# Loading the first tile of an interleave kernel by eight 16-row DMAs

## The chip, the cores and the metric

The kernel runs on one core of a Trainium2 chip. Times are device microseconds. A time quoted for a kernel is the median of its unprofiled runs; a "span" is that of one profiled run and is some 2 us shorter. A "row" below is one packet of 32 KiB: one partition of a tile, moved by one of the core's 16 DMA engines. SBUF is the on-chip memory that holds the tiles, HBM the memory off the core that holds x, y and the result.

## The reference

```python
batch, seq, dim = 32, 256, 1024          # x and y: float32, 32 MiB each
result = np.zeros((batch, seq, dim * 2), dtype=np.float32)
result[..., 0::2] = x
result[..., 1::2] = y
```

There is no arithmetic: 64 MiB are read and 64 MiB written.

## The kernel before

```python
P, WL, WS = 128, 8192, 4096
xpool, ypool, opool = ...                # two buffers each          [cut]
nc.vector.memset(zero, 0.0)              # 16x128
nc.scalar.dma_start(out=first, in_=zero) # 8 KB into out; overwritten later
for lw in lwidths:                       # eight tiles of 128 x 8192
    xs = dataclasses.replace(xf, offset=start, ap=[[lw, P], [1, lw]])
    ys = ...                                                        # [cut]
    nc.sync.dma_start(out=xtile, in_=xs) # 4 MiB, 128 rows of 32 KiB
    nc.sync.dma_start(out=ytile, in_=ys)
    while soff < lw:                     # two halves of 4096 columns
        nc.vector.tensor_copy(out=otile[:, 0::2], in_=xsub)
        nc.vector.tensor_copy(out=otile[:, 1::2], in_=ysub)
        nc.scalar.dma_start(out=os_, in_=otile)   # 4 MiB
```

After compiling, the very first load is moved ahead of the barrier at the program's start. Loads go through SyncE's queue (q1), stores through ScalarE's (q10); both use the same 16 DMA engines (2304 and 2336 packets, 49.9% and 49.5% of the engines' time in the span).

## Time and profile before

| | before |
|---|---|
| median of the first five runs | 315.93 us (315.54 to 316.48) |
| span of the profiled run | 313.8 us |
| DMA engines busy | 99.4% of the span |
| rows for each DMA engine | 256, of 1.213 us each: 310.5 us |
| first x tile landed, first y tile landed | 12.27 us, 21.97 us |

### The profile page before, as it was taken

How to read it: one execution, taken by the hardware profiler on the slowest of the kernel's cores; microseconds unless marked ns; L12 is line 12 of the kernel's file. 1: busy time of each engine (PE TensorE's matmuls, PEld its weight loads, DVE VectorE, ACT ScalarE, POOL GpSimd, SP SyncE). 2: the span in 40 equal slices, each digit the busy share in tenths (PEclk: the TensorE clock that was granted, in tenths of full speed). 3: DMA queues.
4: the chain of work that ended last, by engine and by line, in shares of the span. 5: the costliest groups of instructions: out<-in, count | busy, mean ns of one | idle time of the engine just before them, and what ended most of it. 6: DMA issues, size and time to landing. Idle time of an engine off the chain costs nothing.

```text
span 313.8 us, 152 instructions
## 1 busy us (share of the span) xinstructions
DVE 72.8 (23%) x33; POOL 0.2 (0%) x4
## 2 busy tenths in 40 slices
DVE  0433002231032410325003150130501305023500
POOL 0000000000000000000000000000000000000000
DMA  8999999999999999999999999999999999999997
GB/s 339 464 405 397 468 401 464 405 464 405 464 405 464 405 459 409 451 418 451 418 434 434 430 439 426 443 413 455 401 468 401 468 401 468 401 468 401 464 405 334
DMA packets 4640, 134.23 MB, mean 428 GB/s; under 512 B 528, under 2 KB 544, under 8 KB 544
## 3 DMA queue, kind: packets, MB, share of 16 engines
q1 hardware_dynamic: 2304, 67.11, 49.9%
q10 hardware_dynamic: 2336, 67.12, 49.5%
HBM read 67.11 MB, written 67.12 MB: 428 GB/s over the span
## 4 chain that ended last, share of the span: by engine, by line
DMA 83%; DVE 11%; DVEq 1%; issue 0%
DMA out_dram<-otile 76%; DMA ytile<-in_y_dram 7%; DVE otile L71 6%; DVE otile L70 5%; DVEq L83 1%; DVEq L70 0%
## 5 line engine op out<-in xcount | busy, mean ns | idle before, releaser
L70 DVE COPY otile<-xtile 128x4096 f32<-128x4096 f32 x16 | 36.6, 2295 | 184.9 <-DMA out_dram<-otile 173.7
L71 DVE COPY otile<-ytile 128x4096 f32<-128x4096 f32 x16 | 36.6, 2292 | 39.8 <-DMA ytile<-in_y_dram 39.8
L45 DVE MEMSET zero<- 16x128 f32 x1 | 0.2, 165 | 0.9 <-PEq L119 0.9
L119 POOL MEMSET const-bfloat16-1.0<- 128x1 bf16 x1 | 0.1, 102 | 0.0
L119 POOL MEMSET const-uint8-127<- 128x1 uint8 x1 | 0.1, 102 | 0.0
L119 POOL MEMSET const-float32-0.0<- 128x1 f32 x1 | 0.1, 99 | 0.2 <-issue 0.2
L119 POOL MEMSET const-float32-1.0<- 128x1 f32 x1 | 0.1, 99 | 0.0
## 6 DMA issues: line engine op xcount, KB each, us to landing
out_dram<-otile ACTq DMA_DIRECT2D x16, 4096.0 KB, 29.1
xtile<-in_x_dram SPq DMA_DIRECT2D x8, 4096.0 KB, 43.6
ytile<-in_y_dram SPq DMA_DIRECT2D x8, 4096.0 KB, 60.7
out_dram<-zero ACTq DMA_DIRECT2D x1, 8.0 KB, 6.3
```

The source lines that it names most:

```text
L45: nc.vector.memset(zero, 0.0)
L70: nc.vector.tensor_copy(out=otile[:, 0::2], in_=xsub)
L71: nc.vector.tensor_copy(out=otile[:, 1::2], in_=ysub)
L83: tc.compile()
L119: nc = _bacc.Bacc("TRN2", target_bir_lowering=False, num_devices=1)
```

## The change

The first x tile is loaded by eight DMAs. Each has one row for each DMA engine: 16 rows run at a time while x is loaded, and each group of 16 is followed by 16 completion writes. The intent, as the form of the pieces suggests, is that all 16 engines have work after one short DMA and start together. The r-th DMA takes partitions r, 8+r, ... 120+r. Only the first of the eight is moved ahead of the barrier; in the changed kernel's trace SyncE issues the second at 1.21 us.

```diff
-        nc.sync.dma_start(out=xtile, in_=xs)
+        if start == 0:
+            for r in range(P // 16):
+                nc.sync.dma_start(
+                    out=xtile.rearrange("(e r) w -> e r w", r=P // 16)[:, r],
+                    in_=xs.rearrange("(e r) w -> e r w", r=P // 16)[:, r],
+                )
+        else:
+            nc.sync.dma_start(out=xtile, in_=xs)
```

## The prediction

> **What bounds the kernel now.** The kernel moves 64 MiB in and 64 MiB out and has VectorE interleave each pair of tiles in between. I read the page first: the busy shares, the slices, the queues. Then the chain of waits in order of time, then the waits of VectorE, then the issues of SyncE, then windows of the start, and last the records of single DMA packets in the trace, which the page only sums.
>
> The page, its parts 1 to 3:
>
> ```profile
> span 313.8 us, 152 instructions
> ...
> DVE 72.8 (23%) x33; POOL 0.2 (0%) x4
> ...
> DMA  8999999999999999999999999999999999999997
> GB/s 339 464 405 397 468 401 464 405 464 405 464 405 464 405 459 409 451 418 451 418 434 434 430 439 426 443 413 455 401 468 401 468 401 468 401 468 401 464 405 334
> DMA packets 4640, 134.23 MB, mean 428 GB/s; under 512 B 528, under 2 KB 544, under 8 KB 544
> ...
> q1 hardware_dynamic: 2304, 67.11, 49.9%
> q10 hardware_dynamic: 2336, 67.12, 49.5%
> ```
>
> VectorE is busy 23% of the span, the 16 DMA engines 99.4% (the shares of the two queues added), from the first slice to the last. 4640 packets less the 544 small ones are 4096, one for each row of 32 KiB of a tile, so 4096 / 16 = 256 rows for each DMA engine. In the records of single packets, all but a few dozen of these rows take 1.213 us, loads and stores alike: 32768 B / 1.213 us = 27.0 GB/s an engine, 432 GB/s for 16. And 256 x 1.213 = 310.5 us of the span of 313.8. The other 3.3 us are the start (first row at 0.99 us), the longer first row and the completion after the last row (it ends at 312.7). So what binds is the rows that each DMA engine has to work off one after another, and nothing later can make up for time that an engine loses.
>
> The chain in order of time, its first pieces:
>
> ```profile
> by line: DMA out_dram<-otile 76.3%; DMA ytile<-in_y_dram 6.8%; DVE otile L71 5.7%; DVE otile L70 5.1%; DVEq L83 0.7%; issue 0.2%; DVEq L70 0.0%
> ...
> 0.78 21.19 DMA ytile<-in_y_dram
> 21.97 0.02 issue
> 22.00 4.51 DVE otile L71 x2
> 26.50 0.02 issue
> 26.53 40.87 DMA out_dram<-otile
> ```
>
> The chain runs through the first y tile, which queues behind the first x tile on the same 16 engines: x's semaphore is complete at 12.27 us, y's at 21.97, 9.7 us = 8 rows x 1.213 apart. The reader is to see that the chain names y though half of its 21 us is x's transfer. VectorE's waits:
>
> ```profile
> DVE otile L70 <- DMA out_dram<-otile: 173.7, 14, 21.6
> DVE otile L71 <- DMA ytile<-in_y_dram: 39.8, 8, 5.2
> DVE otile L70 <- DMA xtile<-in_x_dram: 11.3, 1, 11.3
> ```
>
> VectorE waits for x only once, 11.3 us at the start: that is the transfer which is changed. SyncE's issues:
>
> ```profile
> 0.00 0.37 SPq L56 DMA_DIRECT2D xtile<-in_x_dram  x1
> 0.78 0.33 SPq L57 DMA_DIRECT2D ytile<-in_y_dram  x1
> 1.16 0.42 SPq L56 DMA_DIRECT2D xtile<-in_x_dram  x1
> 1.63 0.51 SPq L57 DMA_DIRECT2D ytile<-in_y_dram  x1
> 16.80 0.33 SPq L56 DMA_DIRECT2D xtile<-in_x_dram  x1
> ```
>
> An issue costs 0.33 to 0.51 us of SyncE; four tiles are queued by 2.1 us, so the engines are fed for 39 us. And the windows of x's transfer and of y's:
>
> ```profile
> 1.40:11.10 9.70, 0.00 (x0) 0.00 (x0) 1.00 0.91 389
> 11.10:20.80 9.70, 4.50 (x2) 0.00 (x0) 1.00 1.00 432
> ```
>
> (The last two columns are DMA share and GB/s.) y moves at 432 GB/s, x at nearly that from its second row on. Only x's first row is odd: the 16 engines start it between 0.99 and 1.93 us and end it between 2.86 and 3.43, so a row takes 1.5 to 2.3 us here, and the stagger of 0.6 us stays in the later rows.
>
> [...] the small store of 16 rows of zeros has 16 packets of 512 B, and they stand at the row boundaries of 16 different engines (5.27, 5.45, 5.46 us and on). So eight DMAs of 16 rows give each engine eight rows again. [...]
>
> **The change part by part.** Removed: one load of 128 rows. Added: eight of 16 rows, the r-th taking partitions r, 8+r, 16+r, ... 120+r.
>
> - Ports. [...] a row takes 2 x 1.213 = 2.43 us, the eight rows 19.4 in place of 9.7: +9.7 us.
> - [...] with leads of up to 0.6 us I allow -0.2.
> - The first row. [...] If the stagger of 0.6 us halves, the slowest engine gains 0.3: -0.3.
> - Seven more semaphore writes for each engine, some 6 ns each between rows in the records: +0.04.
> - Issues: seven more, 7 x 0.33 to 0.5 = 2.3 to 3.5 us of SyncE, which starts them at 0.78. An engine's first row ends at 2.9 at the earliest and the second DMA is issued at 0.8 to 1.2: fed in time, 0.
> - Waits: the built program has eight completion semaphores in rotation, so the eighth x piece now waits for the first to land, and the first y load waits for the store of zeros (landed 6.3 us after its issue, at 7.4). Six or seven rows per engine are queued meanwhile: 0.
>
> Sum: +9.7 - 0.2 - 0.3 + 0.04 = +9.2 us. All of it lies on the path: DVE's first copy waits for x, y is behind x in the same rings, and the engines are full to the end. So 316.2 + 9.2 = 325.4 us.
>
> **The rivals.**
>
> - Ports don't bind, or buffering hides them: a row stays at 1.21 us. For it: the intent of the change, and that this trace shows no conflict. [...] Time: 316.2 - 0.3 = 315.7 to 316.3.
> - [...]
> - The new waits take over: y's load isn't issued until zeros have landed. If the zeros have their turn after five slow rows, 5 x 2.43 + 1 = 13 us, it is still ahead of x's end at 21. Only if they landed after x's last row would the engines go dry, for 1 to 2 us: 317 to 318 without the port effect.
> - Reads at a pitch of 256 KiB in HBM collide. [...] not expected; it would look like the port effect, but for partition order alone wouldn't matter.
>
> **Range and chances.** The port effect, shared evenly, has some 70%: 324 to 326.5. Partial or unfair sharing some 8%: 319 to 323. No effect, or only starvation at the start, some 22%: 315.5 to 318. Over 2% slower means above 322.5, so slower 0.73, same 0.25, faster 0.02. A range that holds eight in ten has to reach from inside the unlikely low group: 317 to 327.
>
> **What would show it.** Right: x rows of about 2.4 us in the packet records until 21 us; around 216 GB/s at an undiminished DMA share in a window from 3 to 20 us; VectorE's first copy at 21.5 to 22 us and not 12.3, its first copy of y 9.7 us later, near 31.5; the first big store 9 us late; the same shift in each later piece of the chain, and y rows and all later rows at 1.213 again. Wrong: x rows of 1.21 us with the first copy near 12 us (no port limit); half of the engines with fast rows [...]; a gap in the packets between x and y (the semaphore wait); or a shift at the start that shrinks towards the end, which would mean that the engines had slack after all.

The sum came to +9.7 - 0.2 - 0.3 + 0.04 = +9.2 us, on 316.2 us for the kernel before. The factor of 2 on the measured row of 1.213 us and the 0.2 us given back for leads were assumptions, as the halving of the stagger in the third term was. The other two terms leave -0.3 us, or 315.9 us in all. "Port", here and in the expectations below, is only a name for the supposition that the rows of a 16-row piece slow each other where they are written; what would do that, no trace shows. A rival at about 321 us, to which the range of 319 to 323 us belongs, is cut as a whole.

## The result

The changed kernel takes 325.83 us (325.71 to 326.10, five runs) against 315.93 us; the ratio is 1.0315, with a 95% interval from 1.0301 to 1.0329. Ratios here are the mean time of one kernel's fast runs over that of the other's fast runs of the same rounds, so not quite the ratio of the medians quoted. It is slower by 9.9 us; the spans of the two profiled runs (323.65 and 313.85 us) differ by 9.8.

The page of the changed kernel, parts 2 and 3:

```profile
DMA  9999999999999999999999999999999999999997
GB/s 195 211 259 437 450 409 437 454 413 429 454 437 405 454 441 401 454 445 405 445 450 409 437 450 409 437 454 429 413 454 441 401 454 445 405 445 445 405 445 324
DMA packets 4752, 134.23 MB, mean 415 GB/s; under 512 B 640, under 2 KB 656, under 8 KB 656
...
q1 hardware_dynamic: 2416, 67.11, 51.3%
q10 hardware_dynamic: 2336, 67.12, 48.0%
```

The DMA engines look as busy as before, yet the first two slices of the GB/s line show half the rate: a busy engine is not a fast one. The bytes are the same; 112 more small packets are the completion writes of seven more DMAs on 16 engines. Windows of the start:

```profile
1.40:11.10 9.70, 0.06 (x1) 0.00 (x0) 1.00 0.98 207
11.10:20.80 9.70, 0.00 (x0) 0.00 (x0) 1.00 1.00 206
20.80:30.50 9.70, 4.50 (x2) 0.00 (x0) 1.00 1.01 416
```

Before, the first two windows moved 389 and 432 GB/s. Half the rate ends with x's rows, which on the 16 engines end between 20.95 and 22.03 us. VectorE's waits:

```profile
DVE otile L79 <- DMA out_dram<-otile: 172.9, 14, 20.9
DVE otile L80 <- DMA ytile<-in_y_dram: 39.6, 8, 5.2
DVE otile L79 <- DMA xtile<-in_x_dram: 21.5, 1, 21.5
```

Only the single wait for x has grown, from 11.3 to 21.5 us; the others stand within 0.8 us. The start of the chain, asked for the first 40 us:

```profile
1.21 0.09 issue
1.29 0.18 DVE zero L45
1.47 0.02 issue
1.49 8.64 DMA out_dram<-zero
10.13 0.02 issue
10.15 22.44 DMA ytile<-in_y_dram
32.59 0.02 issue
32.61 4.51 DVE otile L80 x2
```

The chain now names the small store of zeros: the first y load is issued at 10.15 us, when the zeros have landed, since it takes over that store's completion semaphore (SyncE waited 4.3 us for it). It looks like a new wait on the path. Whether it is one, an experiment has to say, for y's rows could not have started before x's rows were done. The packet records give the rows themselves. Here x's rows are sorted by start and cut into groups of 16, one row for each engine (the store of zeros and the completion writes are left out):

```
group    before: start, median us      after: start, median us
1        0.99 to 1.93   1.93           1.34 to 2.04    2.16
2        2.86 to 3.43   1.21           3.27 to 4.39    2.54
3                       1.21           5.85 to 6.97    2.49
4                       1.21           8.35 to 9.47    2.55
5                       1.21           10.90 to 12.01  2.39
6 to 8                  1.21           13.30 to 19.52  2.54 to 2.55
y, 1st                  1.21           20.95 to 22.03  1.64
y, 2nd                  1.21           22.89 to 23.52  1.22
```

Every engine is slow, by nearly the same factor, 2.54 / 1.213 = 2.09, and only while x is loaded; so an uneven slowing, which would leave half of the engines with fast rows, is out. Group 5 (the piece r = 4, by the order of issue) is the quickest of the groups 2 to 8. Adding what all rows took above 1.213 us and dividing by 16 engines gives 1.34 us for the kernel before and 10.65 for the changed one: +9.31. The first row starts 0.36 us later: 9.67 of the 9.8 us between the spans.

### The profile page after: what moved, and what is told of

Same layout as the page of the kernel before. It is cut to its first block, busy times and chain, and to the rows that moved or that the text cites. A ratio compares the mean times of both kernels' runs of the same rounds, so it can differ in the third digit from the quotient of the medians.

```text
span 323.7 us, 165 instructions
## 1 busy us (share of the span) xinstructions
DVE 72.8 (22%) x33; POOL 0.2 (0%) x4
## 3 DMA queue, kind: packets, MB, share of 16 engines
q1 hardware_dynamic: 2416, 67.11, 51.3%
## 4 chain that ended last, share of the span: by engine, by line
DMA 83%; DVE 11%; DVEq 1%; issue 0%
DMA out_dram<-otile 74%; DMA ytile<-in_y_dram 7%; DVE otile L80 5%; DVE otile L79 5%; DMA out_dram<-zero 3%; DVEq L92 1%; DVE zero L45 0%; DVEq L79 0%
```

## Experiments

The theory: what costs is which partitions are written at the same time. The expectations call it the port theory. Which partitions would hinder each other was an assumption, which no trace had shown. Rivals: small DMAs cost by their number, issues and waits; the reads collide in HBM; the new wait for zeros holds up y. Each run is timed against the kernel before in its own rounds; the before medians there were 315.65 to 316.29 us.

### Eight DMAs, but of all partitions

```diff
+            for r in range(8):
+                nc.sync.dma_start(
+                    out=xtile[:, r * (lw // 8) : (r + 1) * (lw // 8)],
+                    in_=xs[:, r * (lw // 8) : (r + 1) * (lw // 8)])
```

> The first x tile in eight DMAs again, with the same eight semaphores and the same waits, but each of all 128 rows and 1024 columns (4 KiB a row)[...]. Port theory: a row piece of 4 KiB takes about 0.15 us, x is complete near 12.5 us, total 315.5 to 317.5, same as before. Rival 'eight small DMAs with their issues and waits cost the 10 us': as the changed kernel, near 325.8.

Measured: 317.09 us, ratio 1.0029 (1.0009 to 1.0048). Its first two windows:

```profile
1.40:11.10 9.70, 2.29 (x1) 0.00 (x0) 1.00 0.98 375
11.10:20.80 9.70, 2.30 (x1) 0.00 (x0) 1.00 1.07 461
```

The same number of DMAs with the same waits, the zeros among them, costs about 1 us and not 10, and the rate is near its full value. x was complete at 13.7 us, somewhat later than the 12.5 expected. (VectorE's first copy starts already at 8.7 us, since four pieces make up the first half tile; nothing is gained from it, as the DMA engines, busy for 99.4% of the span here too, set the end.) The number of DMAs is not the cause.

### Sixteen neighbouring partitions

```diff
-                    out=xtile.rearrange("(e r) w -> e r w", r=P // 16)[:, r],
-                    in_=xs.rearrange("(e r) w -> e r w", r=P // 16)[:, r],
+                    out=xtile[r * 16 : (r + 1) * 16],
+                    in_=xs[r * 16 : (r + 1) * 16],
```

> Eight DMAs of 16 rows, but of 16 neighbouring partitions each: [...] nothing else changed. Port theory: a row takes twice the 2.54 us of the changed kernel, about 5 us, eight rows 40 to 41 us, total 345 to 348. Rival 'small DMAs' or 'reads at a pitch of 256 KiB in HBM' (here the reads are contiguous): 325.8 or 316.

Measured: 341.46 us, ratio 1.0791 (1.0764 to 1.0818).

```profile
1.40:11.10 9.70, 0.00 (x0) 0.00 (x0) 1.00 1.01 116
11.10:20.80 9.70, 0.00 (x0) 0.00 (x0) 1.00 0.95 108
```

The rate is a quarter of 432. As many DMAs of the same size, with neighbouring partitions, lose 25 us in place of 10. The time is below the range expected (345 to 348). A row took 4.59 us, not 5: 1.8 times the 2.54 of the changed kernel, not twice, which had been the assumption. Eight rows by 4.59 less 1.213 would be 27 us; the first row took only 3.59, and that of the kernel before is long too (1.93), which leaves some 25.

### Another step, and contiguous reads

Step 4 in place of 8 (partitions q, 4+q, ... 60+q, then the same from 64):

```diff
+                    out=xtile.rearrange("(h e q) w -> h e q w", h=2, q=4)[r // 4][:, r % 4],
+                    in_=xs.rearrange("(h e q) w -> h e q w", h=2, q=4)[r // 4][:, r % 4],
```

> Eight DMAs of 16 rows with partition step 4 in place of 8[...]. Port theory: rows of 2.5 us, total 325 to 326.5, as the changed kernel [...]. If the HBM pitch mattered: clearly different from 325.8, nearer to 316.

Measured: 325.53 us, ratio 1.0297 (1.0279 to 1.0314); rows of 2.5 us.

The SBUF side as in the changed kernel, the reads from 16 neighbouring rows (the first x tile is wrong on purpose):

```diff
-                    in_=xs.rearrange("(e r) w -> e r w", r=P // 16)[:, r],
+                    in_=xs[r * 16 : (r + 1) * 16],
```

> Wrong result on purpose in the first x tile: the SBUF side as in the changed kernel (step 8), the HBM side 16 neighbouring rows for each DMA. Port theory: rows of 2.5 us, 325 to 326.5. Rival 'the reads collide in HBM at a pitch of 256 KiB': rows of 1.21 us, near 316.

Measured: 325.57 us, ratio 1.0297 (1.0281 to 1.0314), rows of 2.5 us. Changing the reads alone changes nothing. So it is the side of the tile, and step 4 and step 8, whose read pitches differ too (128 and 256 KiB), cost the same (325.53 and 325.83 us).

### The order of the pieces

```diff
-            for r in range(P // 16):
+            for r in (0, 4, 1, 5, 2, 6, 3, 7):
```

> The changed kernel with the eight pieces in the order r = 0, 4, 1, 5, 2, 6, 3, 7[...]. Port theory: [...] which made the one row after the change 2.39 in place of 2.55 us in the changed kernel; six more such rows give 6 x 0.15 = 0.9 us: x complete near 22.0, total 324.6 to 325.3. Any theory without ports (size, number, waits, HBM): the same pieces, so 325.8 and rows of 2.54 throughout.

Measured: 324.85 us, ratio 1.0285 (1.0271 to 1.0299); span 322.1 us. The same pieces in another order have rows of 2.33 us (medians of groups 4 to 8: 2.327 to 2.332), where the changed kernel has 2.54 to 2.55 and 2.39 in group 5, the row that the expectation means; that six more such rows would come of the new order was the assumption. x was complete at 21.24 us; that is earlier than the 22.0 expected, mostly since each row gained some 0.2 us and not 0.15. That the order of pieces with equal size matters at all (2.33 against 2.54 us a row) speaks for a cause that depends on which rows are in flight together; which cause is not shown.

### Without the store of zeros

```diff
-    nc.scalar.dma_start(out=first, in_=zero)
```

> The changed kernel without the small store of zeros, so that the first y load, which the chain says waited 8.6 us for that store, is issued near 5 us in place of 10.15. Port theory: no change in the time, 325.3 to 326.2, x complete near 22.9, since six rows for each engine are queued anyway. Rival 'the new wait for zeros holds up y': 317 to 321.

Measured: 325.37 us, ratio 1.0304 (1.0290 to 1.0318). SyncE's issues of this kernel after the x pieces:

```profile
0.00 5.50 SPq L59 DMA_DIRECT2D xtile<-in_x_dram  x8
5.55 0.58 SPq L65 DMA_DIRECT2D ytile<-in_y_dram  x1
```

The first y load is issued at 5.55 us in place of 10.15, and VectorE still starts on x at 22.97 us, on y at 32.44 (changed kernel: 22.96 and 32.61). The wait that the chain of the changed kernel named is worth nothing: y stood in the queue behind x either way. A chain follows the last release before an issue; it does not know that the transfer then queued.

### Half and quarter tiles

Two DMAs of 64 rows at partition step 2, and four of 32 rows at step 4:

```diff
-            for r in range(P // 16):
+            for r in range(2):                       # the other kernel: range(4)
-                    ... "(e r) w -> e r w", r=P // 16)[:, r]
+                    ... "(e r) w -> e r w", r=2)[:, r]   # the other: r=4
```

> Two DMAs of 64 rows at partition step 2[...]. Port theory leaves open how 64 rows are dealt to the engines: [...] as in the changed kernel, 325 to 326; [...] 316 to 317. Theory 'small DMAs cost by their number': 2/8 of the loss, 318.

> Four DMAs of 32 rows at partition step 4[...]. Port theory: [...] as in the alternated order: 324.5 to 326; [...] 316 to 317. Theory 'number of DMAs': half of the loss, 321.

(In each, the first times are for rows that slow each other, the second for rows that do not.)

Measured: 316.52 us, ratio 1.0022 (1.0008 to 1.0036), and 316.83 us, ratio 1.0040 (1.0019 to 1.0061). VectorE's wait for x in the kernel with 64 rows is that of the kernel before:

```profile
DVE otile L79 <- DMA xtile<-in_x_dram: 11.3, 1, 11.3
```

From the third group on, x's rows have a median of 1.21 to 1.22 us in both. So splitting and a partition step as such cost little (0.7 and 1.3 us by the ratios) where a DMA has 64 or 32 rows spread over all 128 partitions. Rows of 1.21 us say that the engines then don't get in each other's way; which engine takes which row, no record shows. Neither kernel is faster than the one before.

### In mid-stream: a load, and a store

The eight pieces at the fifth x tile in place of the first:

```diff
-        if start == 0:
+        if start == 4 * P * lw:
```

> The kernel before, with the eight 16-row pieces at the fifth x tile in place of the first, in mid-stream, where each DMA engine takes a load row and a store row in turn. Port theory: [...] the load rows double as at the start, 324 to 326; [...] the conflict is smaller, 318 to 323. Rival 'the loss belongs to the start, where nothing else is queued': 316 to 317. The pieces' waits in the rotation of semaphores may add a gap of their own, which would show as idle DMA engines.

Loads and stores do mix in mid-stream: in the kernel before, 256 load rows and 272 store rows start between 100 and 140 us. Which load rows would run at the same time was a guess.

Measured: 332.58 us, ratio 1.0518 (1.0500 to 1.0536): more than any theory expected. Two windows of it:

```profile
125.00:165.00 40.00, 9.09 (x4) 0.00 (x0) 1.00 1.00 378
290.00:310.00 20.00, 5.01 (x3) 0.00 (x0) 1.00 0.77 329
```

While the pieces are loaded (first window) the engines are busy and slow: load rows took up to 2.13 us and store rows beside them up to 1.47, and store rows of up to 1.9 us go on after. Later (second window) the engines idle for a quarter of the time (a share of 0.77, where the kernel before has 0.98 and 0.97 in 280 to 290 and 290 to 300 us): the issues of the pieces were spread over 55.9 us by waits for semaphores in use by stores (41.0 us of SyncE's waits before them were ended by a store), and the order of loads and stores behind them is another. The packet records divide the 15.7 us by which the span is longer: summed as above, rows above 1.213 us cost 8.8 us more than in the kernel before (5.5 of them between 130 and 180 us), and the remaining 6.9 us are engines without a row or an uneven end. Why store rows stay slow after the pieces have landed, up to 290 us, is open. That slow rows are not confined to the start is shown.

One store in mid-stream in eight 16-row pieces at step 8, all loads as before:

```diff
-            nc.scalar.dma_start(out=os_, in_=otile)
+            if start == 4 * P * lw and soff == 0:
+                for r in range(P // 16):
+                    nc.scalar.dma_start(
+                        out=os_.rearrange("(e r) w -> e r w", r=P // 16)[:, r],
+                        in_=otile.rearrange("(e r) w -> e r w", r=P // 16)[:, r])
+            else:
+                nc.scalar.dma_start(out=os_, in_=otile)
```

> The kernel before, with one store in mid-stream (the ninth) as eight DMAs of 16 rows at partition step 8; all loads are as before. [...] store rows up to 2.5 us, 320 to 326. If the limit is on writes into the tile alone: 316 to 317.

(The first times are for the case that rows read out of the tile at step 8 are slowed as rows written at that step are.)

Measured: 316.66 us, ratio 1.0019 (0.9993 to 1.0044). In the packet records of its pieces (six looked at, between 184 and 204 us) 15 of the 16 rows of a piece start within 0.4 us of each other and take 1.213 us each; the sixteenth runs about 2 us apart from them and takes at most 1.25. So rows read at the same time from 16 partitions at step 8 are not slowed, where rows written at that step took 2.54 us. The loss shows on writes into the tile.

## Why the prediction was right

**What binds.** Right: the engines stayed full to the end (51.3 + 48.0 = 99.3% of the span), and of the 10.6 us by which the first copy of y was late, 9.9 were still missing at the end.

**Ports, +9.7 us.** Right in size, and in that it is the set of partitions written at a time that matters. Rows took 1.21 us where a DMA had 128 rows, or 64 or 32 spread over all partitions, 2.54 us with 16 at step 8 and 4.59 us with 16 neighbours, with the number of DMAs (eight), the waits and the reads taken out as causes one by one. What it is that such rows share, no record shows. The size was made up otherwise than foreseen: a row took 2.54 us in place of 2.43, so that groups 2 to 8 cost 9.1 us more than seven rows of 1.213, where 8.5 had been set; but the first row, which was long already, grew by only 0.2 (medians 2.16 and 1.93).

**Leads, -0.2 us.** Right in size: group 5 took 2.39 us, 0.15 less than its neighbours, and in the alternated order the rows of groups 4 to 8 took 2.33 us. That leads are the cause is not shown. Not foreseen was the reverse at the end: y's first rows took 1.39 to 1.95 us, some 0.4 us more than 1.21, as they ran beside x's last ones.

**The first row, -0.3 us.** This step failed. The engines start their first row between 1.34 and 2.04 us, a stagger of 0.69 us; before, it was 0.99 to 1.93. The last starter gained nothing, and the first lost 0.36 us. The engines end this row between 3.27 and 4.38 us, 1.1 us apart, where the 0.6 before was to be halved. The issue itself is longer: the first one took 0.57 us in the changed kernel and 0.38 in the kernel with neighbouring partitions, which started its first row at 1.01:

```profile
0.00 0.56 SPq L60 DMA_DIRECT2D xtile<-in_x_dram  x1
```

```profile
0.00 0.38 SPq L60 DMA_DIRECT2D xtile<-in_x_dram  x1
```

(The first line is of the changed kernel, 0.565 us to three places, the second of that with 16 neighbouring partitions; the columns are start and duration.) So it is the partition step, not the 16 rows, that makes an issue longer; in the kernel with contiguous reads, which has the step on the tile's side alone, it took 0.57 us too. The longer issue is 0.19 of the 0.36 us. The rest passed between the end of the issue and the first row: 0.78 us in the changed kernel, 0.62 before. The aim of the change, an earlier start, was missed.

**Semaphores, issues and waits, near 0.** Right: the kernel with eight DMAs of all partitions, which has them all, costs about 1 us; without the zeros nothing changed. An issue of a piece took 0.49 to 0.59 us, more than the 0.33 to 0.5 set, and the engines were still fed in time. The completion writes added 0.07 us of gaps between x's rows, where 0.04 had been set.

**The same shift to the end.** Not quite. The first copy of x began at 22.96 us, not at 21.5 to 22: the last of x's completion signals came 0.9 us after x's last row ended (22.94 and 22.03), against 0.3 in the kernel before (12.26 and 11.94). Why is not shown. The first copy of y is 10.6 us late (32.61 against 22.00), the end 9.9. The kernel before has rows of up to 1.88 us between 26 and 29.5 us, shortly before its first store rows, worth 0.64 us for each engine; the changed kernel has nothing of the kind at any time after x (0.06 us between 23 and 40). Of the experiments, the five with fast first x rows have 0.5 to 0.9 us there, and the four with x rows of 2.3 to 2.5 us have at most 0.06 (that with rows of 4.59 us has 0.07 in all after x and y's first rows). So a part of the loss is given back in a repeatable way. Why these rows are slow in the one sort of kernel and not in the other stays open.

So the prediction of 9.2 us is within 0.7 of the measured 9.9, partly because its misses offset each other. By the row times, summed over an engine: x's rows and y's first cost 9.88 us (10.58 less 0.70, rows before 23 us), where ports and leads together had been set at 9.5; the start cost 0.36 in place of gaining 0.3; the rows after 23 us gave 0.58 back, which had not been foreseen. The rest, up to 9.8 between the spans, lies in what the rows don't contain: the gaps between them and the end.

## What to carry to other kernels

When a load is split, try first the splits that kept the full rate here: by columns (375 and 461 GB/s in the first two windows), or in 32 or 64 rows spread over all 128 (rows of 1.21 to 1.22 us). 16 rows at one step had a half (step 4 or 8: 204 to 213 GB/s) or a quarter (neighbours: 108 to 116) of the full rate of 432. None of the splits that kept the full rate was faster than the single load (317.09, 316.52 and 316.83 us). Judge a DMA-bound stretch by its GB/s and by the time of one packet, not by the busy share, which stayed at 98 to 100% while the rate halved (207 and 206 GB/s). And test a wait that the chain newly names before believing it: here it stood on the chain for 8.6 us and was worth nothing.
